# Three pieces of work moved in the engine queues of a one-core decoder kernel

## The chip, the core and the metric

The kernel runs on one core of a Trainium2 chip. The metric is the device time of one execution in microseconds (us); the engines are PE (TensorE, matmuls; PEld is its weight load), DVE (VectorE), ACT (ScalarE), POOL (GpSimd) and SP (SyncE, which here only issues DMA transfers). A difference of 0.2% is 3.9 us.

## What is computed (the reference, cut)

Two decoder layers on 512 tokens of 1024 features, all in float32. Each layer is a half-step FFN, a token mixer and a second half-step FFN; the mixer of layer 0 is a short gated convolution, that of layer 1 a sparse attention whose logits get a relative-position bias from a table.

```
for i in range(2):
    h = adaln(x, norm_g[i, 0], shift[:, 0], scl[:, 0])     # rms norm, then scale and shift from c
    x = x + 0.5 * gate[:, 0] * swiglu(h, ffn_w_in[i, 0], ffn_w_out[i, 0])
    h = adaln(x, norm_g[i, 1], shift[:, 1], scl[:, 1])
    y = short_conv_mixer(h, ...) if i == 0 else nsa_mixer(h, ..., rel_bias)
    x = x + gate[:, 1] * y
    h = adaln(x, norm_g[i, 2], shift[:, 2], scl[:, 2])
    x = x + 0.5 * gate[:, 2] * swiglu(h, ffn_w_in[i, 1], ffn_w_out[i, 1])
```

## The kernel before, in words

Activations lie transposed, features on the partitions (eight tiles `x[d]` of 128x512, d from 0 to 7). Every float32 product is made of three matmuls on operands split into a high and a low part (`mm3`, L190 to L192: high by high, high by low, low by high). A weight tile is therefore loaded by SP into `wraw` and **split**: ACT writes `whi` (L186), DVE writes `wlo` (L187). Weight buffers come from two places: the pool `wp` (three of `wraw`, `whi`, `wlo` each) and, for every other weight of a stage, a pool of the stage's own (two `wraw`, three `whi` and `wlo`); those are the spare weights here.

The program is one stream of calls. A scheduler turns it into one queue per engine, taken in order; `tc.issue_after(ins)` keeps what is issued inside it behind an instruction, in the scheduler's order only, and `tc.high_priority()` lets work pass ahead. An engine whose next instruction waits holds everything behind it.

Three places matter.

- **The first FFN (`ffn`, s = 0).** `opening` computes six pairs of hidden tiles in the plain way (`pair`: gate and up product, `gu`, then `activate`: silu, product `af`, split into `ahi` and `alo`). Before the last pair it makes sums and differences of the activations (`quarters_again`, DVE L369 to L381, in tiles named `adaraw`, split into `th`, `tl`). The further pairs are made by `seven_products` (Strassen's seven products in place of eight) on sums of weight quarters `qa` and `qb`; `qa` is built by DMA: SP loads two quarters, POOL issues a DMA that adds a third (L564). ACT and DVE split it into `qah`, `qal`, the quarter `a22` into `qbh`, `qbl`. Between the last plain pair and the first seven products lies the output product `y` of the first six hidden tiles: eight outputs d, each with six tiles k.
- **The end of that FFN and the start of the convolution.** The last products `ty` go output by output, first for tokens 0 to 255, then for 256 to 511; `residual` adds each to `x[d]` (DVE L407), ACT squares it, DVE adds the squares up (`nacc`, L267). `Norm.finish` turns them into the factor 1/rms for a half: column sums on PE (`pr<-ones,nacc`, L284), a chain of tiny DVE instructions (L219 to L233), a diagonal `dg` (L291) and a product that spreads it (`pr<-dg`, L292). `Norm.piece` makes the normed tile of one d and one half (DVE `xr` L349, ACT `hhi` L351, DVE `hlo` L352). `head_start` is the first products of the convolution (`hs`): four weights at once, k by k, the first half of the tokens and then the second.
- **The convolution (`conv`).** Step d makes three products `cv` from weights cwi[3d] to cwi[3d+2], and from them, on DVE, the gated convolution `u`, `yc`, `z`, split into `zhi`, `zlo`. After each split `fill` runs some extra jobs: one job `ada_tile` loads 512 KB and reduces it on DVE (L141). The first extra job is `bias_table`, the table for the attention of layer 1: load `onehot` (`oh`) and `rb` (`rbs`), write `rbn` on DVE (L767, L768), four float32 matmuls `pt` (L774, each two rows in the profile), four evictions on ACT (L775), two stores to memory (SP, L776).

Of the kernel before, what the change touches and what calls it, by code (L numbers as in the profile page):

```python
# [13 lines left out]
F32 = mybir.dt.float32  # L14
# [39 lines left out]
def decoder_kernel(ctx, tc, xT, cT, ng, adaw, adab, ffi, ffo, cwi, cw, cwo,  # L54
# [130 lines left out]
    def split(src, hi, lo):  # L185
        nc.scalar.activation(hi, src, AF.Copy)  # L186
        return nc.vector.tensor_tensor(lo, src, hi, ALU.subtract)  # L187
# [50 lines left out]
    class Halves:  # L238
# [3 lines left out]
        def __getitem__(self, i):  # L242
            a, b = i[1].start, i[1].stop
            return self.t[a // HT][:, a % HT:b - a // HT * HT]

    class Norm:
# [110 lines left out]
        @contextmanager  # L357
        def behind(self, act, dve):
            with tc.issue_after(act.ins), tc.issue_after(dve.ins):
                yield  # L360

# [54 lines left out]
    def head_start(nrm, h, jobs, between=None):  # L416
        os = [psum("hs") for _ in jobs]
        for hf, (a, b) in enumerate(HALVES):
# [3 lines left out]
            if hf and between:  # L422
                with nrm.behind(nrm.done[0][0], nrm.diag):
                    between()
# [34 lines left out]
    def ffn_in(f, j, c, own=None, held=3, to=None):  # L459
        return weights(ffi[f, j, c], KD, P, own, held, to=to)  # L460
# [6 lines left out]
    class Hidden:  # L467
# [4 lines left out]
        def keep(self, af):  # L472
            hi = self.fa.tile([P, T], F32R, name="ahi", tag="a")
            lo = self.fa.tile([P, T], F32R, name="alo", tag="a")
            split(af, hi, lo)
# [22 lines left out]
    def opening(f, nrm, hid, hp, tt, soon):  # L498
        with ExitStack() as es:
# [23 lines left out]
            for j in range(FIRST, last + 1):  # L523
                if j == last:
                    nrm.quarters_again(tt, [from_.tile([P, D], F32, name="adaraw", bufs=n) for from_, n in ((ada, 2), (ada, 2), (cd, 2), (cd, 2))])
                hid.activate(*pair(f, j, h, own, None, True, 2))
                fill()

    def ffn(s, f, nrm, nxt, w0, ahead, extra=(), soon=()):
        with ExitStack() as es:  # L530
# [12 lines left out]
            def seven_products(j):  # L543
# [25 lines left out]
                with nrm.behind(*nrm.done[1]) if j == nj and not first else nullcontext():  # L569
                    nc.vector.tensor_tensor(qbs[0], halves[1], raw[:, 0], ALU.add)  # L570
                    nc.vector.tensor_tensor(qbs[1], qbs[0], raw[:, 1], ALU.add)
                split(raw, whi, wlo)
                if qa is halves:
                    for n, q in enumerate(qa):
                        split(q, ah_[:, n], al_[:, n])
                else:
                    split(qa, ah_, al_)
                split(a22, bh_[:, 0], bl_[:, 0])
                if first:
                    for n, q in enumerate(qb):  # L580
                        split(q, bh_[:, n + 1], bl_[:, n + 1])
                else:
                    split(qb, bh_[:, 1:3], bl_[:, 1:3])
# [116 lines left out]
    def conv(s, nrm, nxt, extra, w0, ahead, own):  # L700
        with ExitStack() as es:
# [7 lines left out]

            each = spread(extra, 4 * KD + KD - 3)  # L710
# [5 lines left out]
            for d in range(KD):  # L716
# [25 lines left out]
                rest = split(z, hi, lo)  # L742
# [17 lines left out]
    def bias_table():  # L760
        with tc.tile_pool(name="bt", bufs=1) as bt:
            oh = bt.tile([33, TBL], F32, name="oh")
            nc.sync.dma_start(oh, onehot)
            rbs = bt.tile([32, 16], F32, name="rbs")
            nc.sync.dma_start(rbs, rb)
            rbn = bt.tile([33, 16, NR], F32, name="rbn")
            nc.vector.memset(rbn, MASK)  # L767
            nc.vector.tensor_scalar(rbn[0:32], rbs[:, :, None].to_broadcast([32, 16, NR]), -1.0, None, op0=ALU.mult)  # L768
            rbf = rbn.rearrange("p h r -> p (h r)")
            for A in range(2):  # L770
                ts = bt.tile([P, TBL], F32, name="ts")
                for c in range(2):
                    o = psum("pt")
# [661 lines left out]
```

## Time and profile before

| | |
|---|---|
| median of 3 runs | 1950.26 us (1948.86 to 1951.85) |
| the profiled execution's own time | 1948.08 us |
| its span | 1946.3 us |
| busy over the span | PE 97%, PEld 89%, DVE 81%, ACT 46%, POOL 13% |
| granted TensorE clock, mean | 0.990 |
| moved by DMA | 325.07 MB, mean 167 GB/s |

The profile is of one execution. In its views a row that begins with a time is an instruction: start (us), duration, engine, line, operation, output and inputs, and in brackets how long the engine stood idle before it and what ended that. "issue" means that nothing the profile shows was waited for. In the table of stretches the number before the DMA share is the granted TensorE clock.

### The profile page before, as it was taken

What the parts mean: (1) busy time and instruction counts of PE and PEld (TensorE: products, weight loads), DVE (VectorE), ACT (ScalarE), POOL (GpSimd) and SP (SyncE); (2) the same over time, 40 slices, a digit from 0 to 9 for tenths busy, and PEclk for the clock granted to TensorE, in tenths of its full rate; (3) what the DMA queues carried; (4) which work ended last, traced back from release to release, by engine and by line L of the source; (5) the groups of instructions that cost most, each with busy time, mean ns of one, the idle gap of its engine ahead of it and who ended that gap; (6) DMA issues with size and microseconds to landing.
All of it is one profiled execution on the core that took longest, in us unless ns stands there. A gap on an engine that the chain in (4) does not pass through costs nothing.

```text
span 1946.3 us, 34305 instructions
## 1 busy us (share of the span) xinstructions
PE 1889.5 (97%) x13321; PEld 1740.8 (89%) x13321; DVE 1585.3 (81%) x2771; ACT 898.4 (46%) x1471; POOL 248.7 (13%) x346
## 2 busy tenths in 40 slices
PE   6989999989999999999999999999999899999999
PEld 4979899868889898989989898999888689898989
DVE  8869788858789797988979798887898978685966
ACT  3425353422236343534635253464777766353532
POOL 0011111000011111110111110000344530000100
PEclk9999999989999999999999999999999999999999
DMA  8577667437656777763576775234322315664731
GB/s 316 194 239 195 216 179 222 144 109 251 214 184 173 205 216 229 196 210 120 147 231 198 226 195 170 98 102 146 88 72 68 104 49 141 173 164 130 192 106 66
DMA packets 126879, 325.07 MB, mean 167 GB/s; under 512 B 15435, under 2 KB 16203, under 8 KB 126716
## 3 DMA queue, kind: packets, MB, share of 16 engines
q1 hardware_dynamic: 95628, 244.13, 37.1%
q0 software_dynamic: 31088, 78.76, 17.9%
q8 instruction: 104, 1.70, 0.4%
q14 instruction: 59, 0.48, 0.1%
HBM read 314.18 MB, written 3.15 MB: 163 GB/s over the span
## 4 chain that ended last, share of the span: by engine, by line
PE 82%; DVE 8%; issue 4%; DMA 3%; POOL 2%; ACT 1%; SPq 0%; DVEq 0%; POOLq 0%; ACTq 0%
PE gu L192 12%; PE gu L190 12%; PE gu L191 12%; PE y L190 7%; PE y L191 7%; PE y L192 7%; PE hs L190 2%; PE hs L191 2%; PE hs L192 2%; PE cv L190 2%; PE cv L191 2%; PE cv L192 2%; PE ty L191 2%; PE ty L190 2%; PE ty L192 2%
## 5 line engine op out<-in xcount | busy, mean ns | idle before, releaser
L186 ACT ACTIVATE whi<-wraw 128x1024 fp32r<-128x1024 f32 (+1 forms) x268 | 262.1, 982 | 410.7 <-PE y L191 210.6
L187 DVE TENSOR_TENSOR wlo<-wraw,whi 128x1024 fp32r<-128x1024 f32 (+1 forms) x268 | 303.5, 1136 | 33.2 <-ACT whi L186 32.3
L190 PE MATMUL y<-ahi,whi 128*128 128x512 f32 x576 | 224.7, 393 | 5.4 <-ACT ahi L186 5.4
L191 PE MATMUL y<-alo,whi 128*128 128x512 f32 x576 | 223.7, 392 | 0.5 <-DVE alo L187 0.5
L192 PE MATMUL y<-ahi,wlo 128*128 128x512 f32 x576 | 223.1, 390 | 0.0
L192 PE MATMUL gu<-hhi,wlo 128*128 128x256 f32 x728 | 201.3, 277 | 0.9 <-DVE wlo L187 0.9
L190 PE MATMUL gu<-hhi,whi 128*128 128x256 f32 x728 | 201.3, 277 | 0.0
L191 PE MATMUL gu<-hlo,whi 128*128 128x256 f32 x728 | 201.2, 276 | 0.0
L141 DVE CUSTOM_DVE_ANT_0 adaraw<-adaraw,cond 128x1024 f32<-128x1024 f32 x144 | 173.4, 1221 | 32.1 <-DMA adaraw<-in_adaw 31.7
L564 POOL DMA_DIRECT2D qa<-in_ffi x70 | 84.6, 1208 | 697.4 <-DMA qa<-in_ffi 236.7
L192 PE MATMUL gu<-th,qal 128*128 128x256 f32 x584 | 161.3, 276 | 0.6 <-DVE qal L187 0.6
L190 PE MATMUL gu<-th,qah 128*128 128x256 f32 x584 | 161.4, 276 | 0.0
L191 PE MATMUL gu<-tl,qah 128*128 128x256 f32 x584 | 161.2, 276 | 0.0
L192 PE MATMUL gu<-th,qbl 128*128 128x256 f32 x584 | 161.2, 276 | 0.0
L191 PE MATMUL gu<-tl,qbh 128*128 128x256 f32 x584 | 161.2, 276 | 0.0
L190 PE MATMUL gu<-th,qbh 128*128 128x256 f32 x584 | 161.2, 276 | 0.0
L192 PEld LDWEIGHTS gu<-hhi,wlo 128*128 128x128 f32 x728 | 136.6, 188 | 1.2 <-DVE wlo L187 1.2
L190 PEld LDWEIGHTS gu<-hhi,whi 128*128 128x128 f32 x728 | 136.7, 188 | 0.5
L191 PEld LDWEIGHTS gu<-hlo,whi 128*128 128x128 f32 x728 | 136.6, 188 | 0.5
L186 ACT ACTIVATE qbh<-a 128x512 fp32r<-128x512 f32 x73 | 46.2, 633 | 195.7 <-PE gu L191 187.1
L190 PEld LDWEIGHTS y<-ahi,whi 128*128 128x128 f32 x576 | 107.8, 189 | 32.0 <-ACT ahi L186 10.5
L191 PEld LDWEIGHTS y<-alo,whi 128*128 128x128 f32 x576 | 108.5, 188 | 25.0 <-DVE alo L187 3.2
(320 smaller groups left out, 5615.7 us busy)
## 6 DMA issues: line engine op xcount, KB each, us to landing
wraw<-in_ffi SPq DMA_DIRECT2D x103, 512.0 KB
adaraw<-in_adaw POOLq DMA_DIRECT2D x77, 512.0 KB, 4.4
qa<-in_ffi SPq DMA_DIRECT2D x146, 256.0 KB
wraw<-in_ffo SPq DMA_DIRECT2D x96, 384.0 KB
qa<-in_ffi POOLq DMA_DIRECT2D x70, 512.0 KB, 6.6
adaraw<-in_adaw SPq DMA_DIRECT2D x67, 512.0 KB
a<-in_ffi SPq DMA_DIRECT2D x73, 256.0 KB
wraw<-in_cwi SPq DMA_DIRECT2D x24, 512.0 KB
```

Source lines behind the costliest of these rows:

```text
L141: nc.vector.tensor_tensor_reduce(out=raw, in0=raw, in1=cond, scale=1.0, scalar=0.0, op0=ALU.mult, op1=ALU.add, accum_out=m)
L186: nc.scalar.activation(hi, src, AF.Copy)
L187: return nc.vector.tensor_tensor(lo, src, hi, ALU.subtract)
L190: nc.tensor.matmul(o, sh, mh, start=first, stop=False)
L191: nc.tensor.matmul(o, sh, ml, start=False, stop=False)
L192: nc.tensor.matmul(o, sl, mh, start=False, stop=last)
L564: nc.gpsimd.dma_start(qa, bass.AP(tensor=a21.tensor, offset=a21.offset, ap=[a21.ap[0], [0, 2], a21.ap[1]]), accum_op=ALU.add)
```

## The change

Three edits.

1. `bias_table` becomes a generator with three steps (loads and `rbn`; the first pair of matmuls with its evictions and store; the second), put into the convolution's list of extra jobs at places 1, 12 and 17 in place of the whole at place 0. Its pool lives as long as the activations of the convolution.
2. In the first FFN the operands of the first seven products are issued behind the split of the last plain pair, and both weights of that pair are loaded and split ahead of `quarters_again`.
3. In step 1 of the convolution the weights are issued behind the normed tiles of the first half of the tokens.

```
+    @contextmanager
+    def behind(act, dve):
+        with tc.issue_after(act.ins), tc.issue_after(dve.ins):
+            yield
...
-    def pair(f, j, h, own=None, gate=None, halves=False, held=3):
+    def pair(f, j, h, own=None, gate=None, halves=False, held=3, ready=None):
...
-            w = gate if gate and not c else ffn_in(f, j, c, own if c else None, held)
+            w = ready[c] if ready else gate if gate and not c else ffn_in(f, j, c, own if c else None, held)
...
+                ready = None
                 if j == last:
+                    ready = [ffn_in(f, j, c, own if c else None, 2) for c in range(2)]
                     nrm.quarters_again(tt, ...)
-                hid.activate(*pair(f, j, h, own, None, True, 2))
+                hid.activate(*pair(f, j, h, own, None, True, 2, ready))
...
+                if j == nj and first:
+                    with behind(*hid.done):
+                        operands(nullcontext)
                 else:
+                    operands((lambda: behind(*nrm.done[1])) if j == nj else nullcontext)
...
+            table = bias_table(pool(h_es, "bt", 1))
+            for n in (1, 12, 17):
+                extra.insert(n, lambda: next(table, None))
             each = spread(extra, 4 * KD + KD - 3)
...
-                        w = weights(cwi[3 * d + c], KD, P, own if (d + c) % 2 else None)
+                        with behind(*nrm.done[0]) if d == 1 else nullcontext():
+                            w = weights(cwi[3 * d + c], KD, P, own if (d + c) % 2 else None)
...
-        w = conv(1, nrm, nxt, [bias_table] + [partial(j, home) for j in upto(4, -6)], w, ffn_ahead(1), ap)
+        w = conv(1, nrm, nxt, [partial(j, home) for j in upto(4, -6)], w, ffn_ahead(1), ap)
```

(`hid.done` holds the two instructions of the last split of a hidden tile; `operands` holds the lines that made and split the seven products' operands, unchanged. In `bias_table` only the two `yield`s and the pool are new.)

What this does to the queues, at three places. First ACT at the end of the opening: `sg` is the silu of the last plain pair, `ahi` its split, `qah` and `qbh` the first operands of the seven products, `whi` the weights of the output product. Before:

```order
L186 ACTIVATE whi<-wraw 128x768
L481 ACTIVATE sg<-gu 128x512
L186 ACTIVATE qah<-qa 128x1024
L186 ACTIVATE ahi<-af 128x512
L186 ACTIVATE qbh<-a_1170 128x512
L186 ACTIVATE whi<-wraw 128x768 x4
```

With the change:

```order
L186 ACTIVATE whi<-wraw 128x768
L482 ACTIVATE sg<-gu 128x512
L186 ACTIVATE ahi<-af 128x512
L186 ACTIVATE qah<-qa 128x1024
L186 ACTIVATE qbh<-a_1170 128x512
L186 ACTIVATE whi<-wraw 128x768 x4
```

`ahi` and `qah` have changed places; the four weight splits stay behind `qah`. On DVE `alo` and `qal` change places in the same way, and the two `wlo` of the last pair stand ahead of most of `quarters_again` where they stood behind it.

Second DVE at the end of the first FFN. `x_88` and `x_89` are the last two of the eight `x[d]`, `rs_i` to `rs_r` the chain of tiny instructions of the first half, `wlo` the split of a spare convolution weight. Before:

```order
L187 TENSOR_TENSOR wlo<-wraw,whi 128x1024
L407 SCALAR_TENSOR_TENSOR x_88<-ty,mods,x_88 128x256
L267 TENSOR_TENSOR nacc<-nacc,sq 128x256
L407 SCALAR_TENSOR_TENSOR x_89<-ty,mods,x_89 128x256
L267 TENSOR_TENSOR nacc<-nacc,sq 128x256
L221 TENSOR_SCALAR rs_j<-rs_i 128x2
L731 MEMSET u 128x2
L267 TENSOR_TENSOR nacc<-nacc,sq 128x256
L224 SCALAR_TENSOR_TENSOR rs_a<-rs_j 128x2
L731 MEMSET u 128x2
L267 TENSOR_TENSOR nacc<-nacc,sq 128x256
L225 TENSOR_TENSOR rs_b<-rs_a,nv 128x2
```

With the change:

```order
L233 SCALAR_TENSOR_TENSOR rs_r_3879<-rs_a,rs_r_3877 128x2
L273 TENSOR_TENSOR nacc<-nacc,sq 128x256
L297 TENSOR_SCALAR dg<-ident,rs_r_3879 128x128
L408 SCALAR_TENSOR_TENSOR x_89<-ty,mods,x_89 128x256
L297 TENSOR_SCALAR dg<-ident,rs_r_3879 128x128
L745 MEMSET u 128x2 x2
L273 TENSOR_TENSOR nacc<-nacc,sq 128x256
L355 SCALAR_TENSOR_TENSOR xr<-x_82,mods,pr 128x256
```

Before, most of the first half's chain, its diagonal and the start of the second half's chain stood behind the last addition, and the first normed tile `xr` 28 rows behind it. Now the diagonal stands around the last addition, and `xr` follows four rows behind it; the chain of the second half runs between the normed tiles of the first. Two `wlo` (of cwi[5] and cwi[7]) have gone from the stretch ahead of this to among the normed tiles of the second half, and so have their `whi` on ACT. On PE the column sums of the first half stand 28 matmuls earlier among the `ty`, and `pr<-dg` of the first half stands ahead of the second half's column sums where it stood behind them. SP issues the loads of `oh` and `rbs` two weight loads earlier.

Third PE in the convolution. Before:

```order
L190 MATMUL hs<-hhi_4070,whi 128x256
L191 MATMUL hs<-hlo_4074,whi 128x256
L192 MATMUL hs<-hhi_4070,wlo 128x256
L774 MATMUL pt<-oh,rbn 128x512 x4
L190 MATMUL cv<-hhi_4067,whi 128x512
L191 MATMUL cv<-hlo_4071,whi 128x512
L192 MATMUL cv<-hhi_4067,wlo 128x512
```

With the change:

```order
L190 MATMUL cv<-hhi_4070,whi 128x512
L191 MATMUL cv<-hlo_4074,whi 128x512
L192 MATMUL cv<-hhi_4070,wlo 128x512
L788 MATMUL pt<-oh,rbn 128x512 x2
L190 MATMUL cv<-hhi_4067,whi 128x512
L191 MATMUL cv<-hlo_4071,whi 128x512
L192 MATMUL cv<-hhi_4067,wlo 128x512
```

The last `hs` is now followed by `cv`. The first pair of `pt` stands behind 120 `cv` matmuls (five weights), the second behind 72 more. On SP the two stores of the table, which stood side by side behind four `adaraw` loads, now stand apart, each between weight loads; and seven weight loads in a row (of cwi[9] to cwi[14] and cwi[16]) stand ahead of the first five `adaraw` loads that follow the two already issued, where there were four (cwi[10], and cwi[12] to cwi[14]). On DVE `rbn` stands behind `u` of step 1 and the first `adaraw` reductions.

More of the change, by code (lines that the diff above doesn't have):

```diff
@@ L354, in piece @@
                 self.done.append((act, dve))
[L357 to L360, printed above, removed]
         def quarters_again(self, tt, raws):
@@ L422, in head_start @@
             if hf and between:
-                with nrm.behind(nrm.done[0][0], nrm.diag):
+                with behind(nrm.done[0][0], nrm.diag):
                     between()
@@ L567, in seven_products, with operands @@
                 nc.sync.dma_start(a22, quart(1, 1))
[L569 to L575, printed above, removed]
-                else:
[L577 to L583, printed above, removed]
+                def operands(after):
+                    with after():
+                        nc.vector.tensor_tensor(qbs[0], halves[1], raw[:, 0], ALU.add)
+                        nc.vector.tensor_tensor(qbs[1], qbs[0], raw[:, 1], ALU.add)
+                    split(raw, whi, wlo)
+                    if qa is halves:
+                        for n, q in enumerate(qa):
+                            split(q, ah_[:, n], al_[:, n])
+                    else:
+                        split(qa, ah_, al_)
+                    split(a22, bh_[:, 0], bl_[:, 0])
+                    if first:
+                        for n, q in enumerate(qb):
+                            split(q, bh_[:, n + 1], bl_[:, n + 1])
+                    else:
+                        split(qb, bh_[:, 1:3], bl_[:, 1:3])
+                if j == nj and first:
+                    with behind(*hid.done):
+                        operands(nullcontext)
+                else:
+                    operands((lambda: behind(*nrm.done[1])) if j == nj else nullcontext)
                 def product(o, w, b):
@@ L758, in decoder_kernel, with bias_table @@
     tbl = dr.tile([2, P, TBL], F32, name="tbl")
[L760 to L773, printed above, removed]
-                    nc.tensor.matmul(o, rbf[:, A * P:(A + 1) * P], oh[:, c * T:(c + 1) * T], start=True, stop=True)
-                    nc.scalar.activation(ts[:, c * T:(c + 1) * T], o, AF.Copy)
-                nc.sync.dma_start(tbl[A], ts)
+    def bias_table(bt):
+        oh = bt.tile([33, TBL], F32, name="oh")
+        nc.sync.dma_start(oh, onehot)
+        rbs = bt.tile([32, 16], F32, name="rbs")
+        nc.sync.dma_start(rbs, rb)
+        rbn = bt.tile([33, 16, NR], F32, name="rbn")
+        nc.vector.memset(rbn, MASK)
+        nc.vector.tensor_scalar(rbn[0:32], rbs[:, :, None].to_broadcast([32, 16, NR]), -1.0, None, op0=ALU.mult)
+        rbf = rbn.rearrange("p h r -> p (h r)")
+        yield
+        for A in range(2):
+            ts = bt.tile([P, TBL], F32, name="ts")
+            for c in range(2):
+                o = psum("pt")
+                nc.tensor.matmul(o, rbf[:, A * P:(A + 1) * P], oh[:, c * T:(c + 1) * T], start=True, stop=True)
+                nc.scalar.activation(ts[:, c * T:(c + 1) * T], o, AF.Copy)
+            nc.sync.dma_start(tbl[A], ts)
+            yield
     def nsa_in(c, own=None, held=2):
```

8 lines of the change are left out of this document (4 added, 4 removed).

## The prediction

> **What bounds the kernel now.** I read the page first, then the list of what PE waited for, then stretches of time around the three places that the change touches, then the instructions there. The page:
>
> ```profile
> span 1946.3 us, 34305 instructions
> PE 1889.5 (97%) x13321; PEld 1740.8 (89%) x13321; DVE 1585.3 (81%) x2771; ACT 898.4 (46%) x1471; POOL 248.7 (13%) x346
> ```
>
> PE is busy for 97% of the span, so only what makes PE wait, or run slowly, can be won. What it waited for, longest first (total, times, longest), the rows that fall in the touched places:
>
> ```profile
> PE pt L774 <- issue: 8.5, 1, 8.5
> PE y L190 <- ACT ahi L186: 5.4, 2, 4.7
> PE gu L192 <- DVE wlo L187: 0.9, 1, 0.9
> ```
>
> The two longest waits of PE in the program are the bias table and the first output product. In stretches (length, busy time of PE, PEld, DVE, ACT, POOL, then granted clock, DMA share, GB/s) one sees what a wait costs afterwards:
>
> ```profile
> 86.00:97.00 11.00, 10.65 (x92) 10.65 (x93) 7.78 (x13) 1.97 (x3) 1.80 (x3) 1.00 0.83 257
> 106.00:111.00 5.00, 4.54 (x13) 3.64 (x14) 3.83 (x7) 0.84 (x1) 0.59 (x1) 0.61 0.78 195
> 380.00:390.00 10.00, 5.40 (x22) 4.21 (x21) 8.50 (x41) 2.68 (x7) 0.00 (x0) 0.66 0.19 66
> 412.00:428.00 16.00, 7.72 (x10) 3.02 (x11) 10.90 (x19) 3.17 (x5) 0.00 (x0) 0.55 0.79 254
> 440.00:555.00 115.00, 115.00 (x509) 95.24 (x508) 91.67 (x141) 29.23 (x35) 2.08 (x2) 1.00 0.70 240
> ```
>
> After the waits of 4.7 and 8.5 us the granted clock is 0.61 and 0.55; after the wait of 0.9 us, which lies in the first stretch, it stays 1.00. From 440 on the convolution keeps PE busy without a gap. So each of the three places costs idle time and a slow restart. I call them A (first output product), B (norm ahead of the convolution) and C (bias table).
>
> **A: the split of the last plain pair goes ahead of `qah`, and the pair's weights ahead of `quarters_again`.** PE, then ACT, then DVE:
>
> ```profile
> 97.08 0.39 PE L191 MATMUL y<-alo,whi 128*128 128x512 f32 x1
> 100.06 0.39 PE L192 MATMUL y<-ahi,wlo 128*128 128x512 f32 x1
> 105.11 0.80 PE L190 MATMUL y<-ahi,whi 128*128 128x512 f32 x1 [4.67 <-ACT ahi L186]
> 109.99 0.40 PE L190 MATMUL y<-ahi,whi 128*128 128x512 f32 x1
> 103.48 1.06 ACT L186 ACTIVATE qah<-qa 128x1024 fp32r<-128x1024 f32 x1 [10.15 <-DMA a<-in_ffi]
> 104.45 0.61 ACT L186 ACTIVATE ahi<-af 128x512 fp32r<-128x512 f32 x1
> 85.08 1.22 DVE L187 TENSOR_TENSOR wlo<-wraw,whi 128x1024 fp32r<-128x1024 f32 x1
> 97.36 0.69 DVE L483 TENSOR_TENSOR af<-sg,gu 128x512 f32<-128x512 f32 x1 [3.51 <-PE gu L192]
> 104.57 1.23 DVE L187 TENSOR_TENSOR qal<-qa,qah 128x1024 fp32r<-128x1024 f32 x1 [6.53 <-DMA a<-in_ffi]
> 107.71 0.75 DVE L659 SCALAR_TENSOR_TENSOR x<-y,mods,x 128x512 f32<-128x512 f32 x1 [0.71 <-PE y L192]
> 109.58 0.95 DVE L187 TENSOR_TENSOR wlo<-wraw,whi 128x768 fp32r<-128x768 f32 x1
> ```
>
> `af` is ready at 98.05, but its split `ahi` starts only at 104.45, since ACT holds `qah` ahead of it, and `qah` waits 10 us for a DMA that nothing on PE needs yet. Thirteen matmuls lie between the rows at 97.08 and 100.06, 0.23 us apart; the next was due at 100.29. The tenth from there starts at 109.99 where nine steps of 0.23 would put it at 102.36: 7.63 us lost. The 0.92 us at 86.35 is the last pair's `wlo`, which DVE made at 85.08 behind nine instructions of `quarters_again`; with the change it is made ahead of them. Removed: 0.92 + 7.63 = 8.55 us.
>
> What is late next: PE starts `y` at 97.08 - 0.92 - 0.23 (one `y` matmul no longer goes ahead) = 95.93. `af` comes as much earlier, 96.2 to 96.9; `ahi` then ends at 97.5 and `alo`, as large as `af`, at 98.2. PE wants them for k = 5 after fifteen matmuls, at 99.4: no wait. But `qah` still waits for its DMA, and the four `whi` of outputs d = 3 and later stay behind it. Output 3 begins at 95.93 + 54 x 0.23 = 108.35 and needs its `wlo` two matmuls on, at 108.8. Before, that `wlo` came 5.01 us after the start of `qal`; take off the 0.71 us of waiting in front of `x` and 0.69 for `alo`, which has gone ahead: it starts at 104.57 + 3.61 = 108.18 and ends 0.95 later, at 109.1. So a wait of 0.3 us. It grows if `qa` comes later: the two `wlo` now ahead of `quarters_again` push its last instructions back by 2 x 1.22 = 2.4 us, and the loads of `qa` go into memory that these instructions read. Against this, one weight load has left the stretch in which the DMA share is 0.83. New wait 0 to 2.7 us; I take 1.0, nearer to the end at which the DMA and not DVE decides, since ACT stood 10 us for that DMA. A: -7.6, bounds -8.6 and -5.2 (2.7 of wait and 0.7 of clock). The later `th` and `tl` are covered by `y`, eight outputs of eighteen matmuls, 33 us, which they don't feed.
>
> **B: two weight splits leave the stretch ahead of the norm, and the first half's factor is finished earlier.** PE, then DVE; the last row is the same `pr<-dg` elsewhere at full clock:
>
> ```profile
> 379.93 0.28 PE L192 MATMUL ty<-ahi,tl 128*128 128x256 f32 x1
> 382.17 0.61 PE L284 MATMUL pr<-ones,nacc 128*128 128x1 f32 x4 [1.97 <-DVE nacc L267]
> 384.30 1.22 PE L292 MATMUL pr<-dg,ones 128*128 128x256 f32 x2 [1.52 <-DVE dg L291]
> 386.64 1.22 PE L190 MATMUL hs<-hhi,whi 128*128 128x256 f32 x4 [1.11 <-ACT hhi L351]
> 390.05 0.28 PE L190 MATMUL hs<-hhi,whi 128*128 128x256 f32 x1
> 390.17 0.28 PE L191 MATMUL hs<-hlo,whi 128*128 128x256 f32 x1
> 380.24 0.48 DVE L407 SCALAR_TENSOR_TENSOR x<-ty,mods,x 128x256 f32<-128x256 f32 x1
> 383.97 0.28 DVE L291 TENSOR_SCALAR dg<-ident,rs_r 128x128 f32<-128x128 f32 x1
> 383.22 0.17 DVE L221 TENSOR_SCALAR rs_j<-rs_i 128x2 int32<-128x2 int32 x1
> 398.73 0.86 DVE L349 SCALAR_TENSOR_TENSOR xr<-x,mods,pr 128x256 f32<-128x256 f32 x2
> 399.78 0.88 DVE L352 SCALAR_TENSOR_TENSOR hlo<-xr,mods,hhi 128x256 fp32r<-128x256 f32 x2 [0.19 <-ACT hhi L351]
> 579.14 0.70 PE L292 MATMUL pr<-dg,ones 128*128 128x256 f32 x2
> ```
>
> Before, PE waits first for the second half's squares, then for the first half's diagonal. With the change that diagonal's last part follows the last addition (380.24 and 0.48 long): 380.72 for 383.97, so everything from `pr<-dg` on moves by 3.25 us. What DVE must do before that addition becomes less: two splits of 1.22 us go, about ten tiny instructions of at most 0.17 us come. The second part is the clock: the thirteenth `hs` starts at 390.05, 3.41 us after the first, with one pair `pr<-dg` between; at full steps of 0.12 us it is 12 x 0.12 + 0.70 = 2.1. Together with the 0.5 us on the first `pr<-dg` (1.22 against 0.70) up to 1.8 us more, if the clock holds.
>
> The gaps left to PE are about 0.9 us ahead of `pr<-dg` and under 1 us ahead of `hs`, like the one of 0.92 us after which the row above shows 1.00. In the Trainium skill's page "TensorE: Matmul & The Clock Gate", section "Part 1: The HAM clock gate", the clock falls only after an idle window of about 3.4 us, and comes back after about as long of work, with windows that run freely. By that rule B would be 5.05. The trace agrees so far as it goes: 0.61 after 4.67 us, 1.00 after 0.92.
>
> Against it stand the chain of the second half, which now runs between the normed tiles of the first (eleven of at most 0.17 us), and the two splits (1.22 us of DVE, 1.06 of ACT each) among those of the second. DVE needs (0.86 + 0.88) / 2 = 0.87 us for a normed tile, PE uses it in twelve matmuls, 1.44 us, so these 4.3 us fit into the 16 x 0.57 us that PE gives, but the second half's `pr<-dg` may wait up to 0.5. B: -4.4; bounds -3.0 and -5.1; I take it between, since only one such short gap is in the rows.
>
> **C: the table leaves the seam between `hs` and `cv`.**
>
> ```profile
> 411.52 0.28 PE L192 MATMUL hs<-hhi,wlo 128*128 128x256 f32 x1
> 420.28 7.16 PE L774 MATMUL pt<-oh,rbn 33*128 33x512 f32 x8 [8.48 <-issue]
> 427.38 0.79 PE L190 MATMUL cv<-hhi,whi 128*128 128x512 f32 x1
> 431.11 0.39 PE L190 MATMUL cv<-hhi,whi 128*128 128x512 f32 x1
> 409.57 1.23 DVE L187 TENSOR_TENSOR wlo<-wraw,whi 128x1024 fp32r<-128x1024 f32 x1 [8.91 <-ACT whi L186]
> 418.62 0.27 DVE L767 MEMSET rbn<- 33x256 f32 x1
> 419.90 0.28 DVE L768 TENSOR_SCALAR rbn<-rbs 32x256 f32<-32x256 f32 x1
> ```
>
> The list says "issue", but the end of the wait lies on DVE: `rbn` is finished at 420.18, and PE starts at 420.28. DVE had the four weight splits and the whole of step 0 (`u` to `zlo`) ahead of `rbn`. The first `cv` was due at 411.64 and started at 427.38: 15.74 us. Its weight was split at 410.8, so with the change it starts when `hs` ends. The nine `cv` matmuls up to 431.11 took 3.73 us where 9 x 0.23 = 2.07 is their pace: 1.66. Together 17.4 us. The eight rows of `pt` come back later: they took 7.16 us at a clock of 0.55, and half, 3.6, is their price at 1.00. C: -13.8; the bound on the weak side is the cold price, 7.16, and -10.2.
>
> Moved with it: `rbn` (0.55 us of DVE), four evictions on ACT, two small loads, two stores. DVE reaches `rbn` some 9 us into the convolution, 18 us before the first `pt`; ACT is busy for 29 of 115 us. The stores are queued on SP ahead of weight loads (cwi[20] behind the first), and wait there for the evictions; those loads serve weights two steps or more away. The five `adaraw` loads now stand behind seven weight loads, so DVE may stand for some 5 us at the third reduction, with the splits of cwi[11] and later behind it; PE wants cwi[11] seven weights, 38 us, after the start.
>
> **Sum.** 7.6 + 4.4 + 13.8 = 25.8 us off the profiled execution's 1948.08 (1946.3 of span and 1.8 around it): 1922.3. The median of the runs is 2.2 above that execution, so 1950.26 - 25.8 = 1924.5.
>
> **Rivals.** *The bubble comes back in the convolution.* DVE stands for `adaraw`, `z` of step 1 is late, and PE waits for its PSUM: one more wait like the present 8.48 us with its 1.66 us of slow restart. For: in the second to last stretch above DMA has a share of 0.79. Against: the slack of 38 us. 1950.26 - 25.8 + 10.1 = 1934.6.
>
> *A stays bound by the DMA of `qa`.* If it lands 3 us later, outputs 3 and on wait about that long, and the clock falls again: A gives 3 and not 7.6, 1929.1. For: the 2.4 us above. Against: the load that left.
>
> *Slower: the convolution becomes bound by its loads.* DVE has 115 - 91.67 = 23.3 us to spare in the seven steps from 440 to 555, 3.3 each. If the later `adaraw` loads hold DVE for more than that in each of eight steps, PE waits; it decides the sign from 6.5 us on, and at 8 us the kernel takes 1924.5 + 8 x 4.7 = 1962. Against: this very stretch already runs 8 loads of 512 KB per step with PE never waiting, at a DMA share of 0.70.
>
> *It moves nothing*: PE's gain is taken back by loads further on, 1950. Against: after 440 PE is never idle for long up to the end of the convolution.
>
> **How the numbers follow.** Forecast 72%, bubble 13%, DMA of `qa` 8%, slower 4%, nothing 3%. The forecast's own bounds are 8.6 + 5.1 + 13.8 = 27.5 (1922.8, and 1.4 less as the lowest run lies below the median: 1921.4) and 5.2 + 3.0 + 10.2 = 18.4 (1931.9). To hold eight in ten the range takes in the bubble: 1920.5 to 1936. A change of 0.2%, 3.9 us, is about what a measurement can tell: faster 0.93, the same 0.03, slower 0.04.
>
> **What would show it.** PE's list without `pt` and without `y` on `ahi`; `cv` starting within 0.2 us of the last `hs`; `pt` at about 0.45 us a row; from the last `ty` to the first `hs` under 3.5 us; a short wait in `y` for a `wlo`. Wrong would be: a clock under 0.9 after the norm, or a wait of PE over 3 us in `cv`.

## The result, and the profile after

The changed kernel takes 1924.84 us (median of four runs, 1921.55 to 1925.29), the kernel before 1950.63 beside it (1948.86 to 1951.85). The ratio is 0.9865, 95% interval 0.9848 to 0.9882: 26.3 us faster, 23.0 to 29.6. The profiled execution of the changed kernel took 1924.62 us, 23.5 less than that of the kernel before.

The page of the changed kernel, span and engines:

```profile
span 1922.8 us, 34307 instructions
PE 1881.2 (98%) x13321; PEld 1734.8 (90%) x13321; DVE 1584.4 (82%) x2771; ACT 898.7 (47%) x1471; POOL 247.9 (13%) x346
```

The work is the same (13321 matmuls); 23.5 us of span have gone, and only 8.3 of them are busy time of PE (1889.5 before): the rest was idle time. PE's list of waits, the rows that answer to those of before:

```profile
PE y L190 <- ACT ahi L186: 1.2, 1, 1.2
...
PE pr L298 <- DVE u L745: 0.9, 1, 0.9
...
PE hs L190 <- ACT hhi L357: 0.7, 2, 0.4
...
PE y L192 <- DVE wlo L187: 0.6, 2, 0.4
```

The wait of 8.5 us in front of `pt` is gone. The 1.2 us of `y` on `ahi` is not the old 4.7 but a wait at 283.00, in the third output product of the FFN, where there were 0.76 us before. The stretches around the three places, with the clock before the DMA share:

```profile
86.00:97.00 11.00, 11.00 (x93) 10.71 (x92) 8.27 (x14) 2.76 (x5) 2.37 (x3) 1.00 0.82 250
106.00:111.00 5.00, 4.58 (x20) 3.45 (x20) 5.00 (x9) 1.47 (x2) 0.87 (x2) 1.00 0.98 210
370.00:380.00 10.00, 8.55 (x66) 7.73 (x65) 9.35 (x40) 4.22 (x9) 0.00 (x0) 1.00 0.19 66
399.00:415.00 16.00, 16.00 (x76) 13.43 (x76) 15.80 (x27) 5.39 (x7) 0.00 (x0) 1.00 0.74 235
428.00:543.00 115.00, 115.00 (x511) 93.73 (x510) 91.15 (x136) 32.75 (x41) 5.76 (x6) 1.00 0.68 242
```

The clock is 1.00 in all of them, where it was 0.61, 0.66 and 0.55. Place A, on ACT and PE:

```profile
96.36 0.63 ACT L186 ACTIVATE ahi<-af 128x512 fp32r<-128x512 f32 x1 [4.96 <-DVE af L484]
102.14 1.06 ACT L186 ACTIVATE qah<-qa 128x1024 fp32r<-128x1024 f32 x1 [5.15 <-DMA qa<-in_ffi]
...
108.67 0.50 PE L192 MATMUL y<-ahi,wlo 128*128 128x512 f32 x1 [0.42 <-DVE wlo L187]
```

`ahi` no longer stands behind `qah`, which still waits 5 us for its DMA. What is late next is a `wlo` of the output product, by 0.42 us. Place B on PE:

```profile
373.27 0.28 PE L192 MATMUL ty<-ahi,tl 128*128 128x256 f32 x1
374.49 0.70 PE L298 MATMUL pr<-dg,ones 128*128 128x256 f32 x2 [0.94 <-DVE u L745]
375.26 0.61 PE L290 MATMUL pr<-ones,nacc 128*128 128x1 f32 x4
376.30 0.73 PE L190 MATMUL hs<-hhi,whi 128*128 128x256 f32 x4 [0.43 <-ACT hhi L357]
```

The row names the `u` that follows in DVE's queue; what PE waits for is the diagonal `dg`, which DVE ends at 374.44, 0.05 us before. From the last `ty` to the first `hs` it takes 3.03 us instead of 6.71. Place C on PE:

```profile
399.92 0.28 PE L192 MATMUL hs<-hhi,wlo 128*128 128x256 f32 x1
400.04 0.40 PE L190 MATMUL cv<-hhi,whi 128*128 128x512 f32 x1
...
427.04 0.39 PE L192 MATMUL cv<-hhi,wlo 128*128 128x512 f32 x1
427.35 1.98 PE L788 MATMUL pt<-oh,rbn 33*128 33x512 f32 x4
429.26 0.50 PE L190 MATMUL cv<-hhi,whi 128*128 128x512 f32 x1
```

`cv` follows the last `hs` without a gap, and a pair of `pt` takes 1.91 us to the next `cv`, with no wait.

### The profile page after: what moved, and what is told of

It reads as the page before. It is cut to its first block, busy times and chain, and to the rows that moved or that the text cites. A ratio compares the mean times of both kernels' runs of the same rounds, so it can differ in the third digit from the quotient of the medians.

```text
span 1922.8 us, 34307 instructions
## 1 busy us (share of the span) xinstructions
PE 1881.2 (98%) x13321; PEld 1734.8 (90%) x13321; DVE 1584.4 (82%) x2771; ACT 898.7 (47%) x1471; POOL 247.9 (13%) x346
## 4 chain that ended last, share of the span: by engine, by line
PE 82%; DVE 8%; issue 3%; DMA 3%; POOL 2%; ACT 1%; SPq 1%; DVEq 0%; POOLq 0%; ACTq 0%
PE gu L192 12%; PE gu L190 12%; PE gu L191 12%; PE y L190 7%; PE y L191 6%; PE y L192 6%; PE hs L192 2%; PE hs L191 2%; PE hs L190 2%; PE cv L190 2%; PE cv L191 2%; PE cv L192 2%; PE ty L191 2%; PE ty L192 2%; PE ty L190 2%
## 5 line engine op out<-in xcount | busy, mean ns | idle before, releaser
L187 DVE TENSOR_TENSOR wlo<-wraw,whi 128x1024 fp32r<-128x1024 f32 (+1 forms) x268 | 303.3, 1135 | 30.3 <-ACT whi L186 29.6
```

What stands on the lines that cost most here:

```text
L187: return act, nc.vector.tensor_tensor(lo, src, hi, ALU.subtract)
```

## The experiments

**Theory**: the three gains lie in separate stretches and add up; each is a wait of PE with the slow clock behind it. **Rivals**: the gains hang on each other (the table fits only after edit 3; edit 3 alone only lengthens the wait for `rbn`), or what A wins is given back by its DMA. As runs of one kernel lie up to 9 us apart, each run is also read by stages, from the starts of the first PE rows of each stage in its profile: A, from the first `gu` of the opening to the first `gu` of the seven products; the block of seven products behind it; B, from the first `ty` to the end of the head start; C, from there to the first `y` of the convolution.

| kernel | A | block behind | B | C |
|---|---|---|---|---|
| before | 74.41 | 57.23 | 54.98 | 126.24 |
| changed | 66.55 | 58.07 | 50.11 | 113.09 |
| edit 1 alone | 75.08 | 57.23 | 55.43 | 113.09 |
| edit 2 alone | 67.48 | 57.97 | 55.73 | 127.00 |
| edit 3 alone | 73.85 | 57.23 | 50.10 | 126.75 |
| half of edit 2 | 67.61 | 58.11 | 55.13 | 126.44 |
| changed, table early | 65.64 | 57.23 | 50.12 | 122.88 |
| changed, `pt` twice | 66.92 | 58.01 | 51.48 | 119.81 |
| changed, table in one | 67.40 | 58.47 | 51.45 | 112.72 |
| before, filler | 73.94 | 57.23 | 55.42 | 126.11 |
| changed, split table | 67.49 | 58.07 | 51.63 | 111.60 |
| the same, norm filled | 66.95 | 57.96 | 50.11 | 111.61 |
| probes, first / second | 66.55 / 66.28 | 58.00 / 58.21 | 51.34 / 50.13 | |

**Edit 1 alone.** Edits 2 and 3 are undone in the changed kernel:

```
-                    ready = [ffn_in(f, j, c, own if c else None, 2) for c in range(2)]
...
-                if j == nj and first:
-                    with behind(*hid.done):
-                        operands(nullcontext)
-                else:
+                if True:
...
-                        with behind(*nrm.done[0]) if d == 1 else nullcontext():
+                        if True:
                             w = weights(cwi[3 * d + c], KD, P, own if (d + c) % 2 else None)
```

> The kernel before with edit 1 alone (the bias table in three steps in the convolution; the first output product and the norm as before). My theory: the three gains lie in different stretches and add up, so this one gives C as the trace of the changed kernel has it: 126.24 us from the first cv due to the output product of the convolution become 113.1, 13.2 us less, 1937.4. PE's waits for y on ahi (about 4.7) and for dg (about 1.5) are still there, and pt costs about 2 us a pair with no wait. Rival one, the gains depend on each other: the table only fits into the convolution because edit 3 has put the weight loads in another order, and without it PE waits in cv; then the gain is 8 us or less and PE's list shows a cv or pt wait of over 2 us. Rival two, the table is worth nearly all: 20 us or more, and the other two edits little.

Measured: 1934.95 against 1948.66, ratio 0.9922 (0.9910 to 0.9934), 15.2 us. Stage C is 113.09, to the hundredth that of the changed kernel, and PE's list still has the other two waits:

```profile
PE y L190 <- ACT ahi L186: 4.1, 1, 4.1
...
PE pr L298 <- DVE dg L297: 1.5, 1, 1.5
```

C needs neither of the other edits. Both rivals fall.

**Edit 2 alone**, put into the kernel before:

```
+                    ready = [ffn_in(f, j, c, own if c else None, 2) for c in range(2)]
                     nrm.quarters_again(tt, ...)
...
+                if j == nj and first:
+                    with behind(*hid.done):
+                        operands(nullcontext)
```

> The kernel before with edit 2 alone (weights of the last plain pair ahead of the sums, operands of the seven products behind the split of that pair). My theory: A alone, 7.9 us as read between the two traces (74.41 us from the first gate product to the end of the first output product become 66.55), 1942.8, with y waiting for a wlo for under 0.5 us and the waits for rbn and dg as in the kernel before. Rival: the stretch is bound by the DMA that builds qa, and part of what is won is given back later in the first FFN, where the changed kernel was 1.2 us longer; then 6 us or less, 1944.5 or more.

Measured: 1944.82, ratio 0.9977 (0.9967 to 0.9986), 4.5 us (2.7 to 6.4). Stage A is 6.93 us shorter, the block behind it 0.74 longer. In its list the table's wait is untouched:

```profile
PE pt L784 <- issue: 8.5, 1, 8.5
...
PE y L192 <- DVE wlo L187: 1.5, 2, 1.1
```

The waits for `wlo` are three times what I expected, and something is given back. The rival is right in part: A is worth less at the end than in its own stage.

**Edit 3 alone**, put into the kernel before:

```
+                        with behind(*nrm.done[0]) if d == 1 else nullcontext():
                             w = weights(cwi[3 * d + c], KD, P, own if (d + c) % 2 else None)
```

> The kernel before with edit 3 alone (weights of step 1 of the convolution behind the normed tiles of the first half; the table at its old place behind the head start). My theory: B alone, 4.9 us, 1945.7. The wait for rbn stays about 8.5 us long, since the four weight splits ahead of rbn on DVE wait for buffers that the last hs release, so rbn moves with PE. Rival: rbn is set by DVE's own work and not by PE; then PE arrives 4.9 us earlier and waits 4.9 us longer, the wait grows to about 13 us and the kernel takes 1950, no change: edit 3 would be worth something only together with edit 1.

Measured: 1944.90, ratio 0.9974 (0.9963 to 0.9985), 5.1 us. Stage B is 50.10, 4.88 less, and C as long as before. Of its list:

```profile
PE pt L776 <- issue: 8.5, 1, 8.5
...
PE y L190 <- ACT ahi L186: 4.2, 1, 4.2
```

PE comes 4.9 us earlier to `pt` and waits no longer for it: `rbn` moves with PE, and the rival falls. By time the three parts give 15.2 + 4.5 + 5.1 = 24.8 us; the whole gave 26.3 (23.0 to 29.6). Within these bounds they add up.

**The table earlier in the convolution** (two numbers of the changed kernel):

```
-            for n in (1, 12, 17):
+            for n in (1, 4, 6):
```

> The changed kernel with the table's steps at places 1, 4 and 6 instead of 1, 12 and 17: the first pair of pt stands behind 24 cv matmuls, the second behind 25 more, and rbn at the same place in DVE's queue. Theory: what cost the wait in the kernel before was that PE reaches pt before DVE reaches rbn. PE is there 24 x 0.23 = 5.5 us after the first cv, rbn is finished 11.4 us after it (411.42 - 400.04 in the changed kernel): a wait of 5.9 us, after which the first pair runs at the low clock (3.6 instead of 1.9 us) and the cv behind it lose 1.5 to 2.5 us: 9 to 10 us more than the changed kernel, 1934, and the second pair waits for nothing. Rival: the wait before came from the whole table standing at the seam between two products, where PE had no other work; a table made in steps inside the convolution is hidden wherever it stands: the same as the changed kernel.

Measured: 1935.38 against 1949.36, ratio 0.9926 (0.9911 to 0.9941). By the ratios that is 11.9 us above the changed kernel; C is 9.79 us longer than there. The first row of the table, and two stretches:

```profile
409.10 3.77 PE L788 MATMUL pt<-oh,rbn 33*128 33x512 f32 x4 [5.81 <-DVE rbn L781]
```

```profile
406.00:408.00 2.00, 0.00 (x0) 0.00 (x0) 2.00 (x5) 0.00 (x0) 0.00 (x0) 0.78 0.56 152
...
414.00:416.00 2.00, 2.00 (x7) 1.52 (x6) 0.00 (x0) 0.00 (x0) 0.00 (x0) 0.50 1.03 420
```

A wait of 5.81 where 5.9 was worked out, named here as DVE's `rbn`. So the wait comes from PE reaching `pt` before DVE reaches `rbn`, wherever that is; standing in steps between other products doesn't hide it. The wait began at 403.3 and the clock fell some 3.8 us later, as the 0.78 shows; the Trainium skill's page "TensorE: Matmul & The Clock Gate", section "Part 1: The HAM clock gate", gives an idle window of about 3.4 us, and this wait agrees.

**The table's matmuls twice** (changed kernel):

```
+                for _ in range(2):
                     nc.tensor.matmul(o, rbf[:, A * P:(A + 1) * P], oh[:, c * T:(c + 1) * T], start=True, stop=True)
```

> The changed kernel with each of the four matmuls of the table done twice into the same place (same result). It prices the pt rows where they stand now, in the running convolution. My theory, the price read from the changed kernel's rows (1.98 us a pair and about 0.1 after it, 4.2 us for all four): 4.0 to 4.4 us more than the changed kernel, 1929. By the prediction's half of the cold price: 3.6 more. Rival: PE has slack in the convolution, being paced by splits and loads, and takes four more matmuls for nothing: 0 to 1 us more; then the term C contains no price for pt at all.

Measured: 1929.91, ratio 0.9898 (0.9885 to 0.9912), by the ratios 6.4 us above the changed kernel; C is 6.72 longer in the profiled execution. The first doubled pair took 3.63 us, 1.72 more than a single one: with the second as long that would be 3.4, a little under the prediction's 3.6. The second took 4.37, and the next twelve `cv` stood 0.43 us apart instead of 0.23:

```profile
451.00:452.00 1.00, 1.00 (x4) 0.50 (x3) 0.83 (x2) 0.94 (x2) 0.00 (x0) 1.00 0.00 0
...
454.00:455.00 1.00, 1.00 (x3) 0.15 (x1) 1.00 (x3) 0.04 (x1) 0.00 (x0) 0.50 0.93 344
...
459.00:460.00 1.00, 1.00 (x4) 0.81 (x3) 0.00 (x0) 0.00 (x0) 0.00 (x0) 0.50 0.94 344
```

PE was busy throughout, and the clock fell to 0.50 all the same. The price of `pt` is real (the rival of slack falls), but my theory that only idling lowers the clock was incomplete. The clock fell at 453.30, 2.82 us after the second doubled pair began. The next four runs are about that.

**Filler work in the wait of before** (kernel before):

```
+            fill = psum("fl")
+            for n in range(32):
+                nc.tensor.matmul(fill, h[0][n % KD][:, 0:P], h[0][n % KD], start=True, stop=True)
             for A in range(2):
```

> The kernel before, with 32 matmuls of 128x512 between the last hs and the table (into a PSUM tile that nothing reads): PE still waits for rbn, but does other work for 32 x 0.23 = 7.4 us of that wait, and the idle part falls from 8.5 to about 1.1 us. Theory of the prediction (the slow clock comes from idling alone): the eight pt rows then run at clock 1.00 for about 4 us instead of 7.16 and the cv after them lose nothing, so 3.2 + 1.7 = 4.9 us less than before, 1944-1946. Theory from the run with the table's matmuls done twice, where the clock fell to 0.50 after 3.1 us of pt rows with PE never idle: pt rows don't count as work for the clock gate; eight rows in a row lose it on the way, the last pt rows and the first cv run at 0.50, and the gain is 1 to 3 us. Rival: the price of pt is of another kind than the clock, and nothing changes (0 us).

Measured: 1945.52 against 1950.27, ratio 0.9975 (0.9966 to 0.9984), but spread from 1941.27 to 1950.44 over ten runs. In the profiled execution (1946.67) C won nothing:

```profile
419.78 2.78 PE L778 MATMUL pt<-oh,rbn 33*128 33x512 f32 x4 [1.21 <-issue]
...
425.90 0.79 PE L190 MATMUL cv<-hhi,whi 128*128 128x512 f32 x1
```

```profile
419.00:420.00 1.00, 0.22 (x1) 0.26 (x2) 1.00 (x4) 0.00 (x0) 0.00 (x0) 1.00 0.04 16
...
421.00:422.00 1.00, 1.00 (x2) 0.33 (x1) 1.00 (x3) 0.50 (x1) 0.00 (x0) 0.50 0.88 332
...
427.00:428.00 1.00, 1.00 (x4) 0.81 (x3) 0.00 (x0) 0.53 (x2) 0.00 (x0) 0.50 1.01 393
```

After an idle time of only 1.21 us the clock held for about 1 us of `pt` and then fell; `pt` took 6.12 us instead of 7.10. The other nine executions have a mean clock of 0.995 to 0.996 against 0.992 of this one. By the ratio, 4.9 us (3.1 to 6.6) of the price of C was the clock alone, which is the number of the first theory; the one profile shows what the second one said, and none was taken of an execution with the higher clock. How much it is in one execution stays open.

**The table in one piece inside the convolution** (changed kernel):

```
-            for n in (1, 12, 17):
+            for n in (1, 12, 13):
```

> The changed kernel with the table's second step right behind the first (places 1, 12 and 13 instead of 1, 12 and 17), so that all eight pt rows stand in a row in the running convolution. Theory of the prediction (only idling lowers the clock): the same time as the changed kernel within 0.3 us, four matmuls of two rows in about 3.9 us. Theory that pt rows don't count as work for the clock gate: after 3 to 4 us of them the clock falls to 0.50, and the rows left and the cv behind them lose 2 to 3 us, as after the second doubled pair (12 cv at 0.43 us instead of 0.23); or, where the gate's window falls so that both halves hold some cv, nothing. Then the three steps of the change are more than a matter of rbn being early.

Measured: 1925.45, ratio 0.9872 (0.9855 to 0.9888), not to be told from the changed kernel. All eight rows stand in a row, 3.63 us from 430.12 to the next `cv`, and the clock stayed:

```profile
433.00:434.00 1.00, 1.00 (x3) 0.25 (x2) 1.00 (x2) 0.00 (x0) 0.00 (x0) 1.00 1.03 389
434.00:436.00 2.00, 2.00 (x10) 1.59 (x10) 1.59 (x4) 0.35 (x1) 0.00 (x0) 1.00 0.87 186
```

So 3.6 us of `pt` can pass without a loss, and the distance between the steps is not what makes the gain. Alone, the run doesn't tell the theories of the clock apart. Together with the run of the doubled matmuls it fits the second: there the first doubled pair, just as long, kept the clock, and the second lost it. The difference is where the clock could change, which in each trace is at instants 3.41 us apart (worked out below, at the filled norm): here 2.54 us of `pt` lie ahead of such an instant, in the first doubled pair 2.56, in the second 2.82.

**What in `pt` lowers the clock: two kernels with probes.** To the changed kernel's extra jobs (`pq` is fp32r, `pf` float32, both filled with 0.37; nothing reads the product):

```
+            def probe(name, t, k, times):
+                o = psum("pt")
+                for _ in range(times):
+                    nc.tensor.matmul(o, t[0:k, 0:P], t[0:k], start=True, stop=True)
...
+            for n, j in ((24, lambda: probe("a", pq, 33, 32)), (28, lambda: probe("b", pf, P, 8)), (34, lambda: probe("c", pf, 33, 8))):
+                extra.insert(n, j)
```

> The changed kernel with three probes in the convolution, each with 72 cv matmuls ahead of it and behind it, none of which feeds anything: a, 32 fp32r matmuls on 33 partitions (33x512); b, 8 float32 matmuls on 128 partitions (128x512, two rows each); c, 8 float32 matmuls on 33 partitions, like pt but on constant numbers other than zero. Each lasts over 7 us. What lowers the clock in pt, with PE never idle? If it is the few partitions: the clock falls to 0.50 in a and c, and not in b. If it is float32: in b and c, not in a. If both are needed: in c alone. If it is the data of oh, nearly all zeros: in none of them. The prediction's theory, idling alone, says none as well, and fails with the doubled pairs. At clock 1.00 a takes 7.4 us, b and c about 7.9 each; the kernel takes 23 us more than the changed one, or up to 20 us more than that.

Measured: 1957.98. One stretch inside each probe, in the order a (464.45 to 476.02), b (494.75 to 501.21), c (518.06 to 528.29):

```profile
472.00:474.00 2.00, 2.00 (x6) 1.54 (x5) 0.00 (x0) 0.00 (x0) 0.00 (x0) 0.50 0.76 250
...
500.00:502.00 2.00, 2.00 (x7) 1.00 (x6) 2.00 (x6) 0.13 (x1) 0.00 (x0) 1.00 0.81 268
...
526.00:528.00 2.00, 2.00 (x3) 0.33 (x1) 0.00 (x0) 0.00 (x0) 0.00 (x0) 0.50 0.72 270
```

It is the few partitions: in a and c the clock fell, 2.8 and 3.8 us after the start, and in b it stayed 1.00, float32 as it is. The second kernel has the same places with 32 fp32r matmuls each, on 64 partitions, on 96, and on 128 with 32 output rows:

```
-                    nc.tensor.matmul(o, t[0:k, 0:P], t[0:k], start=True, stop=True)
+                    nc.tensor.matmul(o[0:m], pq[0:k, 0:m], pq[0:k], start=True, stop=True)
...
+            for n, j in ((24, lambda: probe(64, P)), (28, lambda: probe(96, P)), (34, lambda: probe(P, 32))):
```

> The changed kernel with three probes at the places of the run before, each 32 fp32r matmuls of 512 columns (7.4 us at clock 1.00) on constant numbers: the first on 64 partitions with 128 output rows, the second on 96 partitions, the third on 128 partitions with 32 output rows. With 33 partitions the clock fell to 0.50 after 3 to 4 us and stayed there until 3 to 5 us after the probe; with 128 it stayed 1.00. If the gate goes by the share of the array in use, with a bound about half: it falls at 64 or stays by little, stays at 96, and falls at 32 output rows. If it goes by input partitions alone: the third stays 1.00. If anything under 128 counts as idle: it falls in all three.

Measured: 1952.17. A stretch late in each probe:

```profile
476.00:480.00 4.00, 4.00 (x18) 3.00 (x18) 2.54 (x6) 0.16 (x1) 0.00 (x0) 1.00 0.83 249
...
498.00:502.00 4.00, 4.00 (x19) 3.30 (x19) 4.00 (x12) 0.00 (x0) 0.00 (x0) 1.00 0.42 134
...
524.00:526.00 2.00, 2.00 (x10) 0.99 (x9) 2.00 (x3) 0.00 (x0) 0.00 (x0) 1.00 0.92 272
```

None falls. Input partitions decide, with the bound between 33 and 64; few output rows do nothing. The Trainium skill's page "TensorE: Matmul & The Clock Gate", section "Part 1: The HAM clock gate", has the clock set by how busy PE has been recently; here PE is busy for the whole of each probe, as the profile counts it, and the clock falls in two of the six.

**The table from split operands** (changed kernel; `rbh`, `rbl` and `ohr` are fp32r copies of the operands):

```
-                nc.tensor.matmul(o, rbf[:, A * P:(A + 1) * P], oh[:, c * T:(c + 1) * T], start=True, stop=True)
+                nc.tensor.matmul(o, rbh[:, A * P:(A + 1) * P], ohr[:, c * T:(c + 1) * T], start=True, stop=False)
+                nc.tensor.matmul(o, rbl[:, A * P:(A + 1) * P], ohr[:, c * T:(c + 1) * T], start=False, stop=True)
```

> The changed kernel with the table's product made from operands split into a high and a low part like all others (rbn in two parts, the ones and zeros of oh in one), two matmuls of 0.23 us for each float32 matmul of two rows at about 0.5 us. If the price of a pt row where it stands now is the 0.5 us read from the trace, a pair falls from 1.98 us to 4 x 0.23 = 0.92, and the kernel is 2.1 us faster than the changed one: 1922.5. If PE has slack there, no change; if the split of rbn on ACT and DVE holds weight splits behind it, PE waits in cv and it is slower.

Measured: 1925.44, ratio 0.9872 (0.9858 to 0.9887). C is 1.49 us shorter and not 2.1, as a pair now takes 1.12 us to the next `cv` in place of 1.91, and not 0.92; that is less than the time of this kernel can show. Its profile shows something else, at the norm:

```profile
374.94 0.70 PE L298 MATMUL pr<-dg,ones 128*128 128x256 f32 x2 [0.94 <-DVE u L745]
375.71 0.60 PE L290 MATMUL pr<-ones,nacc 128*128 128x1 f32 x4
376.75 0.74 PE L190 MATMUL hs<-hhi,whi 128*128 128x256 f32 x4 [0.44 <-ACT hhi L357]
```

```profile
374.05:377.46 3.41, 2.01 (x11) 1.39 (x11) 2.86 (x14) 1.45 (x4) 0.00 (x0) 1.00 0.00 0
377.46:380.87 3.41, 3.41 (x17) 3.41 (x17) 3.34 (x15) 2.02 (x4) 0.00 (x0) 0.50 0.00 0
380.87:384.28 3.41, 3.41 (x29) 3.36 (x29) 3.22 (x10) 2.34 (x5) 0.00 (x0) 1.00 0.00 0
```

The same waits as in the changed kernel, 0.94 and 0.44, and here the clock falls to 0.50 for 3.41 us.

**The same with the norm's wait filled.** Behind the last `ty` of the first FFN:

```
+            if first:
+                o = psum("fl")
+                for k in range(4):
+                    nc.tensor.matmul(o, a[0][k][:, 0:P], a[0][k], start=True, stop=True)
```

> The changed kernel with the table's matmuls split into high and low parts as in the run above, and four matmuls of 128x512 into a PSUM tile that nothing reads behind the last ty of the first FFN, where PE waits 0.94 us for the diagonal of the norm. In four of five profiled executions with edits 1 to 3 the clock fell to 0.50 for some 3 us after that wait and cost 1.3 us; in one it stayed 1.00. Theory: it falls because idle time and narrow matmuls (the column sums, 128x1) fill too much of one window of the gate; with the wait filled it stays 1.00 and ty to cv takes 50.1 us in place of 51.4: about 1.3 us less than with the split table alone, 1923 to 1924. Rival: the four matmuls (0.92 us) make pr or hs late and cost up to 1 us; or the clock falls all the same and nothing changes.

Measured: 1923.22 (1922.62 to 1927.11), ratio 0.9871 (0.9857 to 0.9884). Stage B is 50.11 and its clock 1.00:

```profile
378.00:380.00 2.00, 2.00 (x19) 2.00 (x18) 1.93 (x11) 1.17 (x3) 0.00 (x0) 1.00 0.00 0
```

But four of the eight profiles with edit 3 and no filler have 50.1 as well, so this execution alone proves nothing; the lowest median of all is not faster than the changed kernel by more than the interval.

The traces say more when they are read between the instants at which the clock can change. In each of the fourteen, all changes of the granted clock lie whole multiples of 3.41 us apart (in the kernel before at 103.09, 109.92, 382.99, 389.81, 413.71 and 430.77). The stretches shown for the split table lie between such instants; at the norm of the changed kernel they are:

```profile
370.98:374.39 3.41, 2.57 (x22) 2.36 (x21) 3.31 (x17) 0.99 (x4) 0.00 (x0) 1.00 0.54 194
374.39:377.80 3.41, 2.81 (x17) 2.19 (x18) 2.86 (x13) 1.71 (x4) 0.00 (x0) 1.00 0.00 0
```

With the split table both waits lie in one stretch, the first of the three shown there: PE is idle for 1.40 us of it and at the column sums, 128x1, for 0.60 more, and behind it the clock is 0.50. In the changed kernel a boundary parts the same two waits, and the clock holds. The eight profiles without filler all go this way: 1.9 to 2.1 us of idle time and column sums in one stretch where the clock fell, at most 1.6 where it held. Over all fourteen traces, from 45 us on and leaving out stretches with matmuls on 33 partitions, the clock held through every stretch with up to 1.74 us of these and fell behind all 21 with 1.79 or more. With the filler the stretch at the norm has 0.5 of idle time and 0.6 of column sums. By this reading the clock holds there wherever the boundary lies; a second execution with the filler was not traced.

**Half of edit 2.** The operands behind the split of the last plain pair, its weights where they were; against edit 2 alone:

```
-                    ready = [ffn_in(f, j, c, own if c else None, 2) for c in range(2)]
```

> The kernel before with half of edit 2: the operands of the seven products behind the split of the last plain pair, but the weights of that pair where they were, behind the sums. Theory: the wait of 0.92 us in the last pair is still there, the wait of y for ahi is gone: 6.93 us (edit 2 alone, first gate product to the end of the first output product) less 0.9, 6.0 us in that stretch, and 1.0 to 1.5 us of waits for wlo in y or less, since DVE is done with the sums 2.4 us earlier. Rival: the weights ahead of the sums are needed as well, since without them af is late and y waits for ahi again: 3 us or less in that stretch.

Measured: 1942.87 against 1949.36, ratio 0.9965 (0.9953 to 0.9977), 6.8 us (4.5 to 9.2): not less than the whole of edit 2. Two rows of PE:

```profile
85.92 0.39 PE L192 MATMUL gu<-hhi,wlo 128*128 128x256 f32 x1 [0.92 <-DVE wlo L187]
...
126.20 0.50 PE L192 MATMUL y<-ahi,wlo 128*128 128x512 f32 x1 [0.56 <-DVE wlo L187]
```

The 0.92 us is back, and the waits for `wlo` in `y` are 0.56 instead of 1.50: stage A comes out the same (67.61 and 67.48). The order of `ahi` and `qah` makes the gain; the earlier weights only move a wait.

## Why the prediction was right, step by step

The forecast, 1924.5 from a sum of 25.8, met the time for the reasons given. By stages over all profiles:

| term | predicted | the two profiles | means over the profiles |
|---|---|---|---|
| A | 7.6 | 7.86 | 74.32 (four without edit 2) - 66.81 (nine with it) = 7.5 |
| B | 4.4 | 4.87 | 55.34 (five) - 50.80 (eight, without the filler) = 4.5 |
| C | 13.8 | 13.15 | 126.61 (before, edits 2 and 3 alone, half of edit 2) - 113.09 (changed, edit 1 alone) = 13.5 |

- **A.** The bound of 8.55 less a new wait for `wlo`, taken as 1.0: that wait was 0.42 and 0.18 in the changed kernel, 1.50 with edit 2 alone. What the prediction left out is that part of the gain is given back: in eight of nine profiles with edit 2 the block of seven products behind is 58.0 to 58.5 us long and not 57.23. The changed kernel waits there for `p` (ACT, 0.35 us at 132.83); that this comes from PE being early is argued only. So A is worth about 6.7 at the end.
- **A, the last pair's weights.** "Removed: 0.92" was true of the row and not of the time: half of edit 2 keeps the wait and is as fast.
- **B.** The chain, the diagonal and the short waits came as worked out, 0.94 and 0.43 us. "If the clock holds" was the open part: it held in the changed kernel's profile, but in four of eight profiles the same waits brought it to 0.50, worth 1.3 us; a clock under 0.9 after the norm was one of the signs that the prediction named for being wrong. So 4.4 met a mean of two outcomes, 5.2 where the clock held and 3.9 where it fell, which depend on where the 3.41 us boundaries lie. The sum by the rule that the prediction cites from the Trainium skill's page "TensorE: Matmul & The Clock Gate", section "Part 1: The HAM clock gate", 5.05, lies near the 4.87 between the profiles before and after, in the second of which the clock held; the four others, where it fell after 0.94 and 0.44 us of waiting, speak against an idle window of 3.4 us as the condition. So did a row of the prediction already: 0.66 in the stretch 380:390 of before, where no wait is longer than 1.97 us.
- **C.** The wait and its cause (DVE reaching `rbn` late) are shown by the early table: 5.81 against 5.9. The price of `pt` was put at half the cold one, 3.6; it is 2 x 1.91 = 3.8. The reason for the cold price was half right: the wait brought the clock down, but it was `pt` itself, on 33 partitions, that kept it there for 7 us.
- **The rivals.** No wait of PE over 0.2 us stands in `cv`, so there was neither the bubble nor a bound by loads; DVE stood 0.88 us for an `adaraw` at 425.92, and nothing on PE waited for it.

The span shrank by 23.5 us and not by the 25.9 of the three stages. In the first FFN behind stage A 1.2 us went: 0.35 is the wait for `p`, 0.40 the longer wait in the third output product, the rest is open. Another 1.3 us stand behind the convolution, without a cause that I can show. The medians of the runs differ by 25.8. That the forecast lies only 0.3 us from the median is luck in part: the interval of the gain reaches 3.3 us to either side, and the 0.8 us that the block behind A gives back was not in the sum.

## What to carry to other kernels

A small step costs what its inputs are late, on the engine that is last to reach them, plus the clock that PE loses while it waits: move the step behind its inputs, not into a gap that looks free. When a wait is taken away, look for the next tensor that is late on the same engine, since a part of the gain may only move there. Short waits close together add up for the clock: here it went by the idle time within one stretch of 3.41 us, not by the longest wait. Keep matmuls on few partitions (33 here) short and between full ones: they cost more than their rows, because they can take the clock with them.

## What the runs showed of the hardware

- Matmuls on 33 partitions let the granted clock fall to 0.50 with PE fully busy, after 2.8 us (fp32r) and 3.8 us (float32), and it came back 4.9 and 3.8 us after the full matmuls began. On 64, 96 and 128 partitions, and with 32 output rows, it stayed 1.00 for over 6 us.
- A float32 matmul of 512 columns took 0.81 us on 128 partitions (8 in 6.46 us), an fp32r one 0.23 (32 in 7.3 to 7.5 us).
- Within a trace the granted clock changed only at instants whole multiples of 3.41 us apart, and these lay elsewhere in the program from one execution to the next. It fell behind stretches of that length with 1.79 us or more of idle time and column sums, and held through those with up to 1.74 (stretches with matmuls on 33 partitions left out).
- The same short waits, 0.94 and 0.44 us with column sums between them, therefore lowered the clock in four profiles of eight: whether they fall into one stretch changes from one execution to the next, and one profile of such a place is not enough.
